# Small GpSimd operations for the decays, late selection, rotary cosine products from PSUM on VectorE, shorter norms, and pads between tiles, in a two-layer hybrid encoder

## The chip, the core and the metric

The kernel runs on one core of a Trainium2 chip. A core has TensorE (PE, matrix products), VectorE (DVE), ScalarE (ACT), GpSimd (POOL) and SyncE (SP, which here only issues transfers), each with an instruction queue of its own that is worked off in order; they meet at semaphores. SBUF is the on-chip memory with 128 partitions; PSUM takes the results of PE. The metric is the device time of one execution in microseconds (us), the median of several runs.

## What is computed

256 tokens of width 1024 in float32 go through two layers and a last RMSNorm:

```python
for l in range(DEPTH):                                   # 2
    h = rmsnorm(x, norm1_g[l])
    (r_q, r_k, r_v, r_g, d_q, d_k, d_v, d_z, d_b, d_a, gate_raw) = split_cols(h @ w_in[l])
    q, k = rotary(r_q), rotary(r_k)                      # 4 heads of 128
    o = retention_bidir(q, k, r_v)                       # fixed decays gamma_h^|n-m|
    y_ret = groupnorm(o) * silu(r_g)
    qkv = silu(centred_dwconv(concat(d_q, d_k, d_v)))    # 5 taps; 8 heads of 128
    dq, dk = l2norm(q part), l2norm(k part)
    g = -exp(a_log) * softplus(d_a + dt_bias)            # decays, per token, head, direction
    od = gated_delta_bidir(dq, dk, dv, beta, g)          # two directions, chunks of 128
    y_dn = rmsnorm(od) * silu(d_z)
    merged = sig(gA) * (y_ret @ w_proj_ret) + sig(gB) * (y_dn @ w_proj_dn)
    x = x + merged @ w_out
    x = x + square(relu(rmsnorm(x) @ w_ff1)) @ w_ff2
return rmsnorm(x, final_g)
```

`rotary` gives `[t1*cos - t2*sin, t1*sin + t2*cos]` of the halves t1, t2 of a head. In each chunk the delta rule needs `dec[i, j] = exp(gc_i - gc_j)` where j is before i (after it, for the other direction) and 0 elsewhere, gc being the running sum of g; it multiplies the k-k products (strictly before) and the q-k products (before or at). Then it solves a unit triangular system of 128 by 128 for each chunk, head and direction.

## The kernel before

**Products.** Weights are float32 and come by SP's transfers in pieces of 512 KB, `wrawc` (128 x 4 x 256) or `wraw` (128 x 2 x 512), three buffers in turn. `split` makes two reduced-precision parts of each piece: `whi` (ACT, L180) and the rest `wlo` (DVE, L181). The activations are kept in such parts too (`hTh`, `hTl` for the first norm's result, `h2h`, `h2l` for the second's, both transposed), and each product is three matmuls: hi*hi, lo*hi, hi*lo. There are two forms. `chan_pair` (L215 to L217) holds a 128 x 128 block of weights in the array and streams 256 tokens past it, 48 matmuls for a pair of output blocks: the names are `pcd` (the convolved columns), `pcrq` (rotary columns), `pcga`, `pcgb` (gates), `pcpr`, `pcpd` (projections; they read `yr` and `yd` in place of hT) and `pcf` (FF1). `tok_chunk` (L197 to L199) holds a block of activations and streams 512 columns of weights: `parv`, `parg`, `padz`, `pawo` (reads `mT`) and `paf` (FF2; reads `fh`, `fl`). There are 4608 of the first kind and 1536 of the second.

**Order.** The code is written by stages, and a scheduler that knows of priorities sets the order on each engine; weight transfers and splits are put ahead of other work. In a layer it goes: norm and transposes; gates and decays; conv columns of half 0 (4 heads), rotary columns beside them; half 1; values; the solve; the levels; outputs; projections; `pawo`; norm; FF1; FF2.

**Decays.** `gates_small` brings the running sums to all partitions by DMA as tiles `E` (128 x 2 directions x 2 chunks x 4 heads x 128, one for each half of the heads). For each direction POOL subtracts the partition's own sum (L330, one 128 x 1024 operation with a broadcast operand), then sets the wrong side to -1e30 (L334), and ACT takes one exponential for each half (L341). `delta_kk` multiplies: `A` from the k-k products, `sA` and E (L448), and E itself becomes the q-k products times E (L450). POOL copies four blocks of A into `W` (L459).

**Norm factors.** `half_inputs` collects squares in `ssq` (DVE L393 adds EPS), takes the power -0.5 on POOL (`powm`, L130, result `rs`), and makes `irk`, `rq` and `sA` on DVE (L398 to L405). `normed` does the same for tokens: ACT squares (L139), DVE adds the two halves and scales (L141, L142), POOL takes the power (L130), DVE scales the tokens (`xn`, L145), PE transposes (`pstn`, L167).

**Rotary.** In `retention`, for each of 16 heads of `pcrq` ACT copies the PSUM block to `ru` (L648), DVE multiplies the two exchanged halves by the sine table into `rw` (L650), POOL multiplies `ru` by the cosine table (L651) and adds (L652).

**Solve and levels.** `delta_solve` gathers the diagonal 32 x 32 blocks through DRAM (`gd`, then `Gm`), sets `X` to -Gm with ones on the diagonal (L468, L469), and runs 30 steps on DVE. X and its transpose go out by DMA (`xd`, `xtd`, L480, L481) and come back as some 40 small transfers into `dd`, `D` and `DT`; `delta_levels` then combines blocks with PE (`ps_y`, `ps_m`).

The parts of the program that the diff touches:

## Time and profile before

| | |
|---|---|
| timed runs (3) | 1135.25 us median, 1132.84 to 1136.71 |
| the profiled execution | 1128.0 us, span 1126.3 us |
| mean granted PE clock | 0.982 |
| busy PE / DVE / ACT / POOL | 1082.3 / 765.7 / 599.5 / 195.2 us |
| weight loads of PE (PEld) | 1003.9 us, beside the matmuls |
| transfers | 188.43 MB, 167 GB/s in the mean |

In the views of the profile, a group of instructions is written as line, engine, operation, output <- inputs, shape; buffer numbers are left out. "Busy" of PE counts a matmul from its start to the start of the next where they overlap, so 96% means that nearly every moment belongs to some matmul. In a window's row stand its limits and length, then for each engine the busy time and the count of instructions, then the clock that PE was granted, the transfers' share and their rate. A wait's row has the waiting instruction, what it waited for, the sum in us, how often, and the longest. A stage can be found in time by its names: the rotary and decay stage of layer 0 lies at 50 to 110 us and of layer 1 at 600 to 680, the levels at 205 to 240 and 760 to 795.

### The profile page before, as it was taken

Reading aid. Unit: us, or ns where it says so; the run is one execution under the profiler, and the core shown is the slowest. Engines: PE = TensorE matmul, PEld = TensorE weight load, DVE = VectorE, ACT = ScalarE, POOL = GpSimd, SP = SyncE. Lnnn points to the kernel's source line nnn. Section 1 sums busy time; section 2 is a strip of 40 time slices with the busy share of each in tenths; the row PEclk is TensorE's granted clock in tenths of the full one; section 3 lists DMA queues with packets and bytes.
Section 4 is the critical chain, followed back from the end, with each engine's and each line's share of the span. In section 5 each row is a group of like instructions: output and inputs, shape, how many; then the busy total and the mean of one; then the engine's idle time right before and its main releaser. Section 6 shows DMA issues by size and latency. Waiting matters only on the chain. (4 is left out here: it accounts for less than half of the span.)

```text
span 1126.3 us, 19629 instructions
## 1 busy us (share of the span) xinstructions
PE 1082.3 (96%) x7564; PEld 1003.9 (89%) x7564; DVE 765.7 (68%) x1359; ACT 599.5 (53%) x1046; POOL 195.2 (17%) x193
## 2 busy tenths in 40 slices
PE   6988999999999999999989899999999999999997
PEld 5988888989999899988879898989999989999885
DVE  4998999646576666644468898994657566666453
ACT  5986654433364566533359865454334556555342
POOL 2065200100002043300020751001001012332000
PEclk9999999989999999999999899999999999999999
DMA  6565675453545466556556556655444565655662
GB/s 211 160 182 157 173 211 150 114 158 97 153 145 183 157 203 182 177 191 211 171 165 177 161 162 193 187 154 135 124 142 113 173 204 165 192 185 188 188 194 104
DMA packets 175759, 188.43 MB, mean 167 GB/s; under 512 B 36240, under 2 KB 137010, under 8 KB 175666
## 3 DMA queue, kind: packets, MB, share of 16 engines
q1 hardware_dynamic: 174288, 185.17, 55.0%
q10 hardware_dynamic: 1378, 2.02, 0.5%
q8 instruction: 59, 0.97, 0.4%
q14 instruction: 34, 0.28, 0.1%
HBM read 181.85 MB, written 5.31 MB: 166 GB/s over the span
## 5 line engine op out<-in xcount | busy, mean ns | idle before, releaser
L181 DVE TENSOR_TENSOR wlo<-wrawc,whi 128x1024 fp32r<-128x1024 f32 x192 | 240.7, 1254 | 117.3 <-ACT whi L180 113.3
L180 ACT ACTIVATE whi<-wrawc 128x1024 fp32r<-128x1024 f32 x192 | 202.7, 1057 | 150.0 <-PE pcpr L216 25.3
L181 DVE TENSOR_TENSOR wlo<-wraw,whi 128x1024 fp32r<-128x1024 f32 x128 | 158.2, 1236 | 111.7 <-ACT whi L180 111.6
L180 ACT ACTIVATE whi<-wraw 128x1024 fp32r<-128x1024 f32 x128 | 135.5, 1059 | 172.3 <-PE paf L199 92.0
L216 PE MATMUL pcf<-h2l,whi 128*128 128x256 f32 x512 | 143.8, 283 | 0.0
L217 PE MATMUL pcf<-h2h,wlo 128*128 128x256 f32 x512 | 143.0, 283 | 0.0
L215 PE MATMUL pcf<-h2h,whi 128*128 128x256 f32 x512 | 142.0, 284 | 0.0
L217 PE MATMUL pcd<-hTh,wlo 128*128 128x256 f32 x384 | 110.8, 292 | 0.9 <-DVE wlo L181 0.9
L215 PE MATMUL pcd<-hTh,whi 128*128 128x256 f32 x384 | 110.3, 291 | 0.0
L216 PE MATMUL pcd<-hTl,whi 128*128 128x256 f32 x384 | 109.8, 287 | 0.0
L199 PE MATMUL paf<-whi,fl 128*128 128x512 f32 x256 | 100.8, 394 | 0.0
L198 PE MATMUL paf<-wlo,fh 128*128 128x512 f32 x256 | 100.7, 394 | 0.0
L216 PEld LDWEIGHTS pcf<-h2l,whi 128*128 128x128 f32 x512 | 98.2, 192 | 0.0
L217 PEld LDWEIGHTS pcf<-h2h,wlo 128*128 128x128 f32 x512 | 98.0, 192 | 0.0
L215 PEld LDWEIGHTS pcf<-h2h,whi 128*128 128x128 f32 x512 | 97.1, 192 | 0.0
L197 PE MATMUL paf<-whi,fh 128*128 128x512 f32 x256 | 90.2, 392 | 0.0
L832 POOL TENSOR_TENSOR fz<-fz 128x256 f32<-128x256 f32 x64 | 66.6, 1042 | 117.7 <-ACT fz L831 116.7
L215 PEld LDWEIGHTS pcd<-hTh,whi 128*128 128x128 f32 x384 | 73.9, 194 | 1.1 <-issue 0.2
L217 PEld LDWEIGHTS pcd<-hTh,wlo 128*128 128x128 f32 x384 | 73.5, 193 | 1.6 <-DVE wlo L181 1.2
L216 PEld LDWEIGHTS pcd<-hTl,whi 128*128 128x128 f32 x384 | 74.1, 193 | 0.4
L363 DVE SCALAR_TENSOR_TENSOR cacc<-pcd,cw,cacc 128x255 f32<-128x255 f32 (+1 forms) x144 | 67.1, 475 | 5.7 <-ACT cac L359 4.7
L197 PEld LDWEIGHTS paf<-whi,fh 128*128 128x128 f32 x256 | 48.1, 188 | 11.0
(268 smaller groups left out, 2637.6 us busy)
## 6 DMA issues: line engine op xcount, KB each, us to landing
wrawc<-in_w_in_dram SPq DMA_DIRECT2D x96, 512.0 KB, 3.8
wrawc<-in_w_ff_dram SPq DMA_DIRECT2D x64, 512.0 KB, 3.7
wraw<-in_w_ff_dram SPq DMA_DIRECT2D x64, 512.0 KB, 3.7
wraw<-in_w_in_dram SPq DMA_DIRECT2D x48, 512.0 KB, 3.7
wrawc<-in_w_proj_ret_dram SPq DMA_DIRECT2D x16, 512.0 KB, 3.4
wrawc<-in_w_proj_dn_dram SPq DMA_DIRECT2D x16, 512.0 KB, 3.4
wraw<-in_w_out_dram SPq DMA_DIRECT2D x16, 512.0 KB, 3.7
E<-rowd SPq DMA_DIRECT2D x16, 256.0 KB, 5.3
```

What stands on the lines that cost most here:

```text
L180: A.activation(hv, raw, AF.Copy)
L181: V.tensor_tensor(lv, raw, hv.bitcast(F32), ALU.subtract)
L197: T.matmul(ps[t], lhsT=a, rhs=wh[:, kk, :], start=k == 0, stop=False)
L198: T.matmul(ps[t], lhsT=a, rhs=wl[:, kk, :], start=False, stop=False)
L199: T.matmul(ps[t], lhsT=b, rhs=wh[:, kk, :], start=False, stop=k == nk - 1)
L215: T.matmul(ps[i], lhsT=wh[:, kk, c], rhs=a, start=k == 0, stop=False)
L216: T.matmul(ps[i], lhsT=wh[:, kk, c], rhs=b, start=False, stop=False)
L217: T.matmul(ps[i], lhsT=wl[:, kk, c], rhs=a, start=False, stop=k == KT - 1)
L363: V.scalar_tensor_tensor(a[:, o], ps[i][:, q], wk(k), a[:, o], ALU.mult, ALU.add)
L832: G.tensor_tensor(z2, z, z, ALU.mult)
```

## The change

Five things:

1. Decays: POOL's four 128 x 1024 subtractions with a broadcast operand in each layer become 32 operations of 128 x 128, one for each chunk, head and direction, that subtract a per-partition value and take the minimum with 0. The selection goes away from in front of the exponential; it stands in `delta_kk`, behind the copies into W, and sets the wrong side of the finished products to 0.
2. Rotary: `ru` is made by one DVE product that reads PSUM and the cosine table; ACT's copy and POOL's product are gone.
3. Norms: the squares are scaled as they are taken, so that one DVE step adds the halves and EPS, in `normed` (first norms) and in the last norm.
4. X is set to zero and ones on POOL ahead of time; five DVE operations copy the strict triangle of -Gm, which replace one whole negation and a memset.
5. Pads: `x1`, `cw1` and `hTl1` are allocated 448, 96 and 128 bytes longer in each partition, and used as before. All that is allocated behind them moves. In the two built programs, the places within a partition, modulo 512 bytes, are:

| tile | before | after |
|---|---|---|
| `whi`, `wlo` | 128 | 224 |
| `hTh`, `hTl`, `h2h`, `h2l` | 128 | 160 |
| `yr`, `yd` | 0 | 160 |
| `mT` | 0 | 160 |
| `fh`, `fl` of layer 0 / layer 1 | 0 / 64 | 160 / 224 |

So the distance weights minus activations, modulo 512, goes from 0 (hT, h2) and +128 (yr, yd) to +64 in all products of 256 columns; in those of 512 columns the distance activations minus weights goes from 0 (hT), -128 (mT, fh of layer 0) and -64 (fh of layer 1) to -64 (hT, mT, fh of layer 0) and 0 (fh of layer 1).

```diff
@@ -58,7 +58,9 @@
 
     SEQ = "11111011101101"
 
-    xh = [hp.tile([P, NT, 512], F32, tag=f"x{j}", name=f"x{j}") for j in range(2)]
+
+    xh = [hp.tile([P, NT * 512 + 112 * j], F32, tag=f"x{j}", name=f"x{j}")[:, :NT * 512]
+          .rearrange("p (t c) -> p t c", t=NT) for j in range(2)]
     cc = cst.tile([P, C_END - C_GAM], F32, tag="cc", name="cc")
     prow = sm.tile([P, 4, P], F32, tag="junk", name="prow")
     rows1, rows2, crow = prow[:16, 0], prow[:34, 1], [prow[:CK * 24, 2 + l] for l in range(DEPTH)]
@@ -105,7 +107,7 @@
 
     gT = cst.tile([P, 16], F32, tag="gT", name="gT")
     gT2 = cst.tile([P, 34], F32, tag="gT2", name="gT2")
-    cw = [cst.tile([P, CK * 24], F32, tag=f"cw{l}", name=f"cw{l}") for l in range(DEPTH)]
+    cw = [cst.tile([P, CK * 24 + 24 * l], F32, tag=f"cw{l}", name=f"cw{l}")[:, :CK * 24] for l in range(DEPTH)]
 
     def columns(dst, src, n):
         ps = aux.tile([P, 512], F32, tag="aux", name="ps_g")
@@ -136,10 +138,9 @@
             ss = sm.tile([P, 2], F32, tag="ss", name="ss1")
             for j in range(2):
                 junk = sm.tile([P, 512], mybir.dt.bfloat16, tag="djunk", name="junk1", bufs=1)
-                A.activation(junk, xh[j][:, t, :], AF.Square, accum_out=ss[:, j:j + 1])
+                A.activation(junk, xh[j][:, t, :], AF.Square, scale=D ** -0.5, accum_out=ss[:, j:j + 1])
             r = sm.tile([P, 1], F32, tag="r1", name="r1")
-            V.tensor_tensor(r, ss[:, 0:1], ss[:, 1:2], ALU.add)
-            V.tensor_scalar(r, r, 1.0 / D, EPS, ALU.mult, ALU.add)
+            V.tensor_scalar(r, ss[:, 0:1], ss[:, 1:2], EPS, ALU.add, ALU.add)
             powm(r, r, 1)
             for j in range(2):
                 V.tensor_scalar(dst[j][:, t, :], xh[j][:, t, :], r, None, ALU.mult)
@@ -218,7 +219,8 @@
         return ps
 
     def halves(tag, p, nm, dt=F32R):
-        return [p.tile([P, 4, S], dt, tag=f"{tag}{j}", name=f"{nm}{j}") for j in range(2)]
+        return [p.tile([P, 4 * S + (32 * j if tag == "hTl" else 0)], dt, tag=f"{tag}{j}", name=f"{nm}{j}")
+                [:, :4 * S].rearrange("p (k s) -> p k s", k=4) for j in range(2)]
 
     hT_hi, hT_lo = None, None
     for l in range(DEPTH):
@@ -326,13 +328,12 @@
                     for c in range(NT):
                         DQ.dma_start(
                             E[:, c], rowd[d, c, d, HH * hf:HH * hf + HH, :].partition_broadcast(P))
-                    i0 = 8 * d + HH * hf
-                    G.tensor_tensor(E, E, gc[:, :, i0:i0 + HH].unsqueeze(3).broadcast_to([P, NT, HH, P]),
-                                    ALU.subtract)
-                    ev = E.rearrange("p c h i -> p (c h) i")
-                    sg = 1 if d == 0 else -1
-                    G.affine_select(ev, ev, pattern=[[0, 8], [sg, P]], base=0, channel_multiplier=-sg,
-                                    compare_op=ALU.is_ge, fill=-1e30)
+
+                    for c in range(NT):
+                        for h in range(HH):
+                            u = 8 * d + HH * hf + h
+                            G.tensor_scalar(E[:, c, h, :], E[:, c, h, :], gc[:, c, u:u + 1], 0.0,
+                                            ALU.subtract, ALU.min)
             Ws = [dl.tile([P, 8, P], F32, tag="W", name="W", bufs=2) for hf in range(2)]
             for hf in range(2):
                 G.memset(Ws[hf], 0.0)
@@ -458,6 +459,11 @@
             for d, b, c in PAIRS:
                 G.tensor_copy(sc["W"][hf][blk[b], :, blk[c]], Av[d][blk[b], :, blk[c]])
             DQ.dma_start(sc["gd"][64 * hf:64 * hf + 64].rearrange("(u b) (j i) -> (b j) u i", b=4, i=32), adg)
+            for d in range(2):
+                ev = E[d].rearrange("p c h i -> p (c h) i")
+                sg = 1 if d == 0 else -1
+                G.affine_select(ev, ev, pattern=[[0, 8], [sg, P]], base=0, channel_multiplier=-sg,
+                                compare_op=ALU.is_ge, fill=0.0)
             q.update(E=E, Av=Av)
 
         def delta_solve():
@@ -465,8 +471,14 @@
             Gm = dl.tile([P, 32, 32], F32, tag="G", name="Gm")
             DQ.dma_start(Gm, sc["gd"].rearrange("q (j i) -> q j i", i=32))
             X = dl.tile([P, 32, 32], F32, tag="X", name="X")
-            V.tensor_scalar(X, Gm, -1.0, None, ALU.mult)
-            V.memset(X.rearrange("p a b -> p (a b)")[:, 0:1024:33], 1.0)
+            xf, gf = (t.rearrange("p a b -> p (a b)") for t in (X, Gm))
+            G.memset(X, 0.0)
+            G.memset(xf[:, 0:1024:33], 1.0)
+
+            for n in (16, 8, 4, 2, 1):
+                xs, gs = (bass.AP(tensor=f.tensor, offset=f.offset + n, ap=[f.ap[0], [66 * n, 16 // n], [32, n], [1, n]])
+                          for f in (xf, gf))
+                V.tensor_scalar(xs, gs, -1.0, None, ALU.mult)
             for j in range(1, 31):
                 n = 31 - j
                 tm = sm.tile([P, 256], F32, tag="stm", name="stm", bufs=1)
@@ -645,10 +657,9 @@
                     ps = chan_pair(wl_[:, off + 256 * i:off + 256 * (i + 1)], hT_hi, hT_lo, "rq")
                     for e in range(2):
                         h = 2 * i + e
-                        A.activation(u[:, h], ps[e], AF.Copy)
+                        V.tensor_tensor(u[:, h], ps[e], rot[:, 0], ALU.mult)
                         for a, b in (halfs, halfs[::-1]):
                             V.tensor_tensor(w_[a, h], ps[e][b], rot[b, 1], ALU.mult)
-                        G.tensor_tensor(u[:, h], u[:, h], rot[:, 0], ALU.mult)
                         G.tensor_tensor(t_[:, h], u[:, h], w_[:, h], ALU.add)
                 qk.append(t_)
             qT, kT = qk
@@ -843,7 +854,7 @@
                 V.scalar_tensor_tensor(xv, ps[t], rr2[:, t:t + 1], xv, ALU.mult, ALU.add)
                 if last:
                     A.activation(fin.tile([P, 512], mybir.dt.bfloat16, tag="fj", name="fj"), xv, AF.Square,
-                                 accum_out=fss[:, t, j:j + 1])
+                                 scale=D ** -0.5, accum_out=fss[:, t, j:j + 1])
                     if j == 0:
                         V.tensor_tensor(xg[:, t, :], xv, fg[:, :512], ALU.mult)
         if last:
@@ -852,8 +863,7 @@
             o = fin.tile([P, NT, D], F32, tag="o", name="o")
             for t in range(NT):
                 rt, ts = r[:, t:t + 1], slice(t * P, (t + 1) * P)
-                V.tensor_tensor(rt, fss[:, t, 0:1], fss[:, t, 1:2], ALU.add)
-                V.tensor_scalar(rt, rt, 1.0 / D, EPS, ALU.mult, ALU.add)
+                V.tensor_scalar(rt, fss[:, t, 0:1], fss[:, t, 1:2], EPS, ALU.add, ALU.add)
                 powm(rt, rt, 1)
                 V.scalar_tensor_tensor(o[:, t, 512:], xh[1][:, t, :], rt, fg[:, 512:], ALU.mult, ALU.mult)
                 A.activation(o[:, t, :512], xg[:, t, :], AF.Copy, scale=rt)
```

The order on POOL in layer 0, from the decays to the rotary sums, before (`rs` is the power that `half_inputs` of half 0 waits for):

```order
L330 TENSOR_TENSOR E<-E,gx 128x1024 x2
L334 AFFINE_SELECT E<-E 128x1024
L330 TENSOR_TENSOR E<-E,gx 128x1024
L334 AFFINE_SELECT E<-E 128x1024
L130 TENSOR_TENSOR rs<-ssq,mh 128x16
L330 TENSOR_TENSOR E<-E,gx 128x1024
L334 AFFINE_SELECT E<-E 128x1024 x2
L651 TENSOR_TENSOR ru<-ru,rot 128x256 x2
L652 TENSOR_TENSOR rT_1059<-ru,rw 128x256 x2
```

and after:

```order
L335 TENSOR_SCALAR E<-E,gx 128x128 x32
L132 TENSOR_TENSOR rs<-ssq,mh 128x16
L663 TENSOR_TENSOR rT_1075<-ru,rw 128x256 x4
L663 TENSOR_TENSOR rT_1710<-ru,rw 128x256 x3
L132 TENSOR_TENSOR rs<-ssq,mh 128x16
L663 TENSOR_TENSOR rT_1710<-ru,rw 128x256
L460 COPY W<-A_730 32x8x32 x2
L465 AFFINE_SELECT E<-E 128x1024
L460 COPY W<-A_731 32x8x32 x2
L465 AFFINE_SELECT E<-E 128x1024
```

The 32 small operations all stand ahead of the first `rs`, where before one subtraction and two selections came behind it; the cosine products are gone, and the four selections come among the copies into W.

The order on DVE in layer 0, from the sum of squares of half 0 (`ssq`) to the first use of its power (`irk`), before:

```order
L393 TENSOR_SCALAR ssq<-ssq 128x16
L363 SCALAR_TENSOR_TENSOR cacc<-pcd_870,cw_104,cacc 128x255
L363 SCALAR_TENSOR_TENSOR cacc<-pcd_870,cw_104,cacc 128x254
L364 TENSOR_TENSOR cacc<-cacc,cac_940 128x254
L181 TENSOR_TENSOR wlo<-wrawc,whi 128x1024
L363 SCALAR_TENSOR_TENSOR cacc<-pcd_964,cw_104,cacc 128x255 x2
L363 SCALAR_TENSOR_TENSOR cacc<-pcd_964,cw_104,cacc 128x254
L181 TENSOR_TENSOR wlo<-wrawc,whi 128x1024
L364 TENSOR_TENSOR cacc<-cacc,cac_1027 128x254
L363 SCALAR_TENSOR_TENSOR cacc<-pcd_965,cw_104,cacc 128x255 x2
L398 TENSOR_TENSOR irk<-ssq,rs 128x8
```

and the end of the same piece after, where `ssq` stands thirty rows further up:

```order
L660 TENSOR_TENSOR ru<-pcrq_1146,rot 128x256
L662 TENSOR_TENSOR rw<-pcrq_1146,rot 64x256 x2
L660 TENSOR_TENSOR ru<-pcrq_1147,rot 128x256
L662 TENSOR_TENSOR rw<-pcrq_1147,rot 64x256 x2
L182 TENSOR_TENSOR wlo<-wrawc,whi 128x1024 x2
L364 SCALAR_TENSOR_TENSOR cacc<-pcd_1216,cw_104,cacc 128x255 x2
L364 SCALAR_TENSOR_TENSOR cacc<-pcd_1216,cw_104,cacc 128x254
L182 TENSOR_TENSOR wlo<-wrawc,whi 128x1024
L365 TENSOR_TENSOR cacc<-cacc,cac_1279 128x254
L364 SCALAR_TENSOR_TENSOR cacc<-pcd_1217,cw_104,cacc 128x255 x2
L364 SCALAR_TENSOR_TENSOR cacc<-pcd_1217,cw_104,cacc 128x254
L399 TENSOR_TENSOR irk<-ssq,rs 128x8
```

Two splits stood between `ssq` and `irk`; now eight do, with the rotary products of four heads (`ru` and `rw`) and another conv block.

The order on SP in layer 0, around the transfers of the solved blocks, before:

```order
L190 DMA wraw<-in_w_in_dram 128x2x512 x8
L208 DMA wrawc<-in_w_in_dram 128x4x256 x5
L480 DMA xd<-X 128x1024
L481 DMA xtd<-XT 128x1024
L502 DMA dd<-xd 32x8x32
L503 DMA dd<-xd 32x8x32
```

and after:

```order
L191 DMA wraw<-in_w_in_dram 128x2x512 x8
L209 DMA wrawc<-in_w_in_dram 128x4x256 x7
L492 DMA xd<-X 128x1024
L209 DMA wrawc<-in_w_in_dram 128x4x256
L493 DMA xtd<-XT 128x1024
L514 DMA dd<-xd 32x8x32
```

`xd` goes out two weight pieces later, and one more piece stands between it and `xtd`.

## The prediction

> **What bounds the kernel now.** I read the page first, then the windows of 50 us, then what PE waited for, then windows of single tiles, then the engines' own timelines at the one stage that has holes. The page says that TensorE is the bound almost everywhere:
>
> ```profile
> span 1126.3 us, 19629 instructions
> PE 1082.3 (96%) x7564; PEld 1003.9 (89%) x7564; DVE 765.7 (68%) x1359; ACT 599.5 (53%) x1046; POOL 195.2 (17%) x193
> ```
>
> The sum below is made against this execution: 1128.0 us, with a span of 1126.3. It lies 7.25 us under the median of the timed runs (1135.25), so I carry the difference over to that median. PE is idle for 1126.3 − 1082.3 = 44 us only; everything else is matmuls, one behind the other. So a change can win in two ways: fill the 44 us, or make a matmul's slot shorter. The windows say where the idle time lies (column PE busy, of 50 us each):
>
> ```profile
> core 0: us, PE busy (x) PEld busy (x) DVE busy (x) ACT busy (x) POOL busy (x), PEclk, DMA share, GB/s
> 50.00:100.00 50.00, 45.45 (x354) 43.51 (x353) 47.32 (x96) 43.02 (x105) 27.77 (x22) 1.00 0.62 179
> 100.00:150.00 50.00, 47.43 (x290) 43.07 (x289) 41.99 (x87) 27.82 (x49) 13.29 (x13) 0.97 0.65 179
> 200.00:250.00 50.00, 46.72 (x420) 45.27 (x419) 25.63 (x50) 21.04 (x39) 4.30 (x4) 0.90 0.50 133
> 600.00:650.00 50.00, 46.08 (x347) 44.96 (x346) 44.91 (x90) 44.08 (x115) 22.33 (x16) 0.90 0.58 170
> 650.00:700.00 50.00, 49.27 (x320) 45.12 (x319) 48.64 (x103) 29.94 (x55) 18.56 (x19) 1.00 0.63 175
> 750.00:800.00 50.00, 47.81 (x415) 45.33 (x414) 29.58 (x63) 21.13 (x39) 3.59 (x4) 0.93 0.57 149
> ```
>
> The rotary-and-decay stage (50 to 150 and 600 to 700) leaves 4.55 + 2.57 + 3.92 + 0.73 = 11.8 us idle: there DVE is 90 to 97% busy and POOL has its only dense stretch. The levels of the block solve (200 to 250, 750 to 800) leave 3.28 + 2.19 = 5.5. The waits of PE name what ended the holes:
>
> ```profile
> engine line waited for: us in total, times, longest us
> PE pstn L167 <- DVE xn L145: 9.3, 4, 4.1
> PE ps_kt L384 <- ACT kq L382: 6.5, 6, 2.2
> ...
> PE ps_m L525 <- DMA DT<-xtd: 3.3, 2, 2.4
> PE pcrq L215 <- DVE cacc L363: 2.8, 3, 2.0
> PE pcrq L215 <- DVE rw L650: 2.6, 1, 2.6
> PE pcrq L217 <- DVE wlo L181: 1.8, 3, 1.1
> ```
>
> **Part 1, the pads.** They move tiles, and add no instruction. By the addresses in the two built programs, the distance between weights and moving data in a partition's memory, taken modulo 512 bytes, was 0 for 3840 of the 4608 products with 256 columns (all that read hT or h2) and +128 for the 768 of `pcpr` and `pcpd`; it becomes +64 for all of them. Did the distance matter before? Both kinds have a window in which PE did nothing else (20 us, busy time, count):
>
> ```profile
> 400.00:420.00 20.00, 20.00 (x169) 20.00 (x168) 2.59 (x7) 1.00 0.68 208
> 340.00:360.00 20.00, 20.00 (x171) 20.00 (x171) 2.50 (x6) 1.00 0.58 181
> ```
>
> The first is `pcf` (distance 0), the second `pcpd` (+128). A window holds every matmul that overlaps it, so the spacing is the window and one matmul's 0.28 us, over the count: 20.28/169 = 120.0 ns and 20.28/171 = 118.6 ns. The same shape at full clock is 1.4 ns cheaper off the distance 0. That is the nearest row for +64, and I take it: 3840 × 1.4 ns = 5.4 us gained, and nothing for the 768.
>
> The 512-column products are the second row that speaks on this: `paf` in layer 0 had the distance −128, in layer 1 −64, and `parv` 0:
>
> ```profile
> 500.00:560.00 60.00, 60.00 (x259) 48.62 (x259) 1.40 (x2) 1.00 0.60 193
> 1050.00:1110.00 60.00, 60.00 (x264) 49.21 (x263) 1.41 (x2) 1.00 0.58 184
> 119.00:125.00 6.00, 6.00 (x28) 4.94 (x28) 0.00 (x0) 1.00 0.56 167
> ```
>
> With 0.39 us for one: 60.39/259 = 233.2, 60.39/264 = 228.8, and 6.39/28 = 228.2 ns (a short window, good to a few ns). Here a distance other than 0 is no cheaper. After the pads the 480 layer-0 products of `paf` and `pawo` go from −128 to −64 (480 × −4.4 ns = −2.1 us), the 96 of `pawo` in layer 1 too (−0.4), `paf` in layer 1 goes to 0 (384 × −0.6 = −0.2), and the 576 on hT go from 0 to −64 (576 × +0.6 = +0.3). Together −2.4; I take −2, with ends −4 and +1.
>
> For the 256-column products the ends are wider, since no row shows +64. Below: a wide slot carries 512 columns in 228.2 ns, so 114.1 for 256 columns; if the pads free the narrow slot of all that it pays beyond this, 3840 × 5.9 + 768 × 4.5 ns = −26 us. Above: in the 512-column rows a distance other than 0 cost 0.6 to 5.0 ns more; half the columns, half of it, 2.5 × 4608 = +12 us.
>
> [...]
>
> **Part 2, the decays.** In the rotary stage POOL and DVE run at once, and DVE pays (start and duration in us, first DVE's rows, then POOL's of the same time):
>
> ```profile
> 61.64 0.41 DVE L364 TENSOR_TENSOR cacc<-cacc,cac 128x254 f32<-128x254 f32 x1
> ...
> 62.36 1.21 DVE L181 TENSOR_TENSOR wlo<-wrawc,whi 128x1024 fp32r<-128x1024 f32 x1
> ...
> 64.00 1.62 DVE L364 TENSOR_TENSOR cacc<-cacc,cac 128x254 f32<-128x254 f32 x1
> 65.55 2.92 DVE L181 TENSOR_TENSOR wlo<-wrawc,whi 128x1024 fp32r<-128x1024 f32 x1
> ...
> 71.49 2.10 DVE L181 TENSOR_TENSOR wlo<-wrawc,whi 128x1024 fp32r<-128x1024 f32 x1
> ...
> 77.31 0.95 DVE L398 TENSOR_TENSOR irk<-ssq,rs 128x8 f32<-128x8 f32 x1
> ```
>
> ```profile
> 63.45 3.93 POOL L330 TENSOR_TENSOR E<-E,gx 128x1024 f32<-128x1024 f32 x2 [50.58 <-DMA E<-rowd]
> ...
> 71.24 1.27 POOL L334 TENSOR_SCALAR_AFFINE_SELECT E<-E 128x1024 f32<-128x1024 f32 x1
> 72.49 3.87 POOL L130 TENSOR_TENSOR rs<-ssq,mh 128x16 f32<-128x16 f32 x1
> ```
>
> The split L181 took 1.21 us alone and 2.92 and 2.10 beside L330; L364, 0.41 at 61.64, took 1.62 at 64.00. And `rs` stands behind the decays in POOL's queue, while DVE's queue stops at `irk` until `rs` is there, with the next splits behind it. This is where `pcrq <- cacc`, `<- wlo` and most of `ps_kt <- kq` come from. The groups give the prices (busy, mean ns):
>
> ```profile
> L330 POOL TENSOR_TENSOR E<-E,gx 128x1024 f32<-128x1024 f32 x8 | 16.4, 2060 | 98.7 <-DMA E<-rowd 96.9 <-DVE cacc L363 1.8
> L651 POOL TENSOR_TENSOR ru<-ru,rot 128x256 f32<-128x256 f32 x16 | 15.4, 970 | 10.4 <-ACT ru L648 10.3
> L334 POOL TENSOR_SCALAR_AFFINE_SELECT E<-E 128x1024 f32<-128x1024 f32 x8 | 11.0, 1384 | 0.0
> L459 POOL COPY W<-A 32x256 f32<-32x256 f32 x16 | 10.3, 641 | 31.0 <-DVE A L448 30.6
> L677 DVE TENSOR_TENSOR sT<-ps_st,cc 128x256 f32<-128x256 f32 x16 | 6.2, 416 | 1.8 <-PE ps_st L675 1.7
> L648 ACT ACTIVATE ru<-pcrq 128x256 f32<-128x256 f32 x16 | 6.0, 374 | 0.0
> ```
>
> Before, each layer had 4 × 2.06 + 4 × 1.38 = 13.8 us of POOL ahead of the last exponential. After, it has 32 small operations of 128x128. No such operation is in the trace: an eighth of L330 is 0.26 us, an eighth with a fixed cost is bounded by the small COPY of 0.64, so 8.3 to 20.5 us; I take 0.4, nearer to the row of the same engine and data, or 12.8 us. The four selections (5.5 us) come behind the W copies, where the window from 100 to 150 above has POOL busy for 13.3 of 50 us; I cost them at nothing. If they were late, the output products behind the levels would wait. Ahead of the first `rs` stood three subtractions and two selections, 8.9 us, and now all 12.8: `rs` comes some 4 us later. But DVE reads it (at `irk`) six splits later, and a split feeds 24 slots of 120 ns: 17 us. So that stop is gone unless the small operations take over (8.9 + 17)/32 = 0.8 us, and what is late next is the first `ps_kk`, whose products now stand later in PE's queue as well.
>
> **Part 3, the rotary products.** 16 `ru` products leave POOL (15.4 us) and 16 copies leave ACT (6.0). DVE gets 16 × 0.416, by L677, which also reads PSUM and one table: 6.7 us, 3.3 in each layer, in a stage where it is the second bound. Against it stands what contention cost DVE there (1.7 + 1.2 + 0.9 us in three of the rows above alone), of which POOL's lost 13 us should take about half. A `pcrq` bank is now let go by three products of one engine in a row, 0.42 + 2 × 0.42 us, where ACT took the first part: up to +0.4 us for each of 8 pairs, hidden where the next pair's bank is free.
>
> Parts 2 and 3 together work on the 11.8 idle us. I take two thirds back, −8. Ends: all of it, −12; and +3, if the 3.3 us of DVE land on the waits of one layer and nothing is won.
>
> **Part 4, norms and X.** Each norm loses one DVE step (the chain ahead of `pstn`, 9.3 us of waits above):
>
> ```profile
> 569.88 0.15 DVE L142 TENSOR_SCALAR r<-r 128x1 f32<-128x1 f32 x1
> ```
>
> Two tokens' tiles in each of two norms, 4 × 0.15, and less than that where the two overlap: −0.5 us. X built by triangles replaces a negation, whose time is covered by PE work, which stands between the solve and the levels. But the order has XT one split and more later, a 512 KB weight transfer between `xd` and `xtd` in SP's queue, and PE's filler ahead of the levels some 3 us of matmuls shorter in layer 0. The wait `ps_m <- DT<-xtd` (3.3) can grow: I take +1, ends −2 and +4.
>
> **The sum.** −5.4 − 2 − 8 − 0.5 + 1 = −14.9: 1113 for the profiled execution, 1120 for the median.
>
> **Rivals.**
> - *The pads do nothing for the 256-column slot.* For it: 228.2 against 228.8 ns in the wide products. Then −8 − 2 − 0.5 + 1 = −9.5: 1126.
> - *The pads do much.* If 118.6 is a quarter of the way out of a collision and +64 leaves it, the slot comes near 114.1 ns: −26 by the end worked out above, with −9.5: 1135.25 − 35.5 = 1100. Against it: no row of this shape is under 118.6.
> [...]
> - *Slower, by the distance.* If +64 behaves as −128 does in the wide products (+5.0 ns in a slot), 4608 × 2.5 to 5.0 ns = +12 to +23, less 9.5: 1138 to 1149. It decides from a slot of about 122 ns; below that the decay stage pays for it.
>
> **Chances.** My forecast 0.37, pads at nothing 0.18, pads much 0.18, eaten gain 0.14, slower by the distance 0.13. A measurement of this kernel tells 0.3% (3.4 us) from no change. The first three are faster, as is the eaten gain in a fifth of its cases: 0.76. The rest of that one is "same", with some of the distance rival: 0.12. Slower keeps 0.12. The range leaves out the upper part of the distance rival and what lies beyond the large gain: 1099 to 1137. The likeliest case alone would have 1113 to 1126: the sum with the decay term at −12 and the levels at −2, or at −2 and +1.
>
> **What would show it.** The spacing of `pcf` in a window of its own (118.6 forecast; 120.0, under 116 or over 122 name a rival). L181 between 60 and 80 us near 1.21 instead of 2.92. PE's waits on `cacc`, `rw`, `wlo` and `kq` in the rotary stage down from 13.7 us to about 5, and no wait on `ps_kk`. L335 at 0.3 to 0.5 us. `ps_m <- DT<-xtd` not over 5 us. What would make me most wrong is a slot that moves by more than 2 ns either way, for there are 4608 of them.

## The result and the profile after

| | before | after | ratio, 95% interval |
|---|---|---|---|
| timed beside each other, first time (4 and 4 runs) | 1134.05 us | 1119.93 us | 0.9877 [0.9849, 0.9906] |
| again on another occasion (11 and 6 runs) | 1130.36 us | 1121.86 us | 0.9920 [0.9896, 0.9943] |
| the profiled executions | span 1126.3 | span 1121.1 | |

The forecast was 1120 us in a range of 1099 to 1137. The time came out, but its large terms did not: the pads brought more than their term and the rotary and decay stage next to nothing, as the profile and the experiments show. The page of after, first lines:

```profile
span 1121.1 us, 19644 instructions
PE 1077.8 (96%) x7564; PEld 998.3 (89%) x7564; DVE 761.1 (68%) x1375; ACT 594.9 (53%) x1030; POOL 217.5 (19%) x237
```

PE's idle time, 1121.1 − 1077.8 = 43.3 us, is what it was (44.0). PE's busy time fell by 4.5. The windows that were shown of before, now of after:

```profile
50.00:100.00 50.00, 45.42 (x362) 44.57 (x361) 39.96 (x80) 41.94 (x98) 35.32 (x37) 0.93 0.64 186
100.00:150.00 50.00, 49.35 (x306) 43.90 (x305) 49.29 (x110) 28.77 (x50) 15.58 (x17) 1.00 0.60 167
200.00:250.00 50.00, 47.30 (x402) 46.49 (x401) 25.17 (x51) 22.20 (x41) 2.64 (x4) 0.83 0.56 147
600.00:650.00 50.00, 46.33 (x380) 45.62 (x378) 40.45 (x80) 43.19 (x105) 34.93 (x36) 0.97 0.66 191
650.00:700.00 50.00, 47.50 (x289) 41.96 (x288) 49.56 (x113) 28.00 (x51) 16.52 (x19) 1.00 0.55 157
750.00:800.00 50.00, 47.86 (x396) 46.59 (x395) 26.87 (x60) 21.65 (x40) 3.31 (x4) 0.82 0.58 153
```

The rotary and decay stage is idle for 4.58 + 0.65 + 3.67 + 2.50 = 11.4 us against 11.8: next to nothing won. And the clock column of the levels fell from 0.90 and 0.93 to 0.83 and 0.82. PE's waits, the first six rows:

```profile
PE ps_kt L385 <- ACT kq L383: 11.8, 7, 4.2
PE pstn L168 <- DVE xn L146: 8.4, 4, 4.9
PE ps_g L114 <- POOL ident L94: 6.0, 1, 6.0
PE ps_y L527 <- DMA dd<-xd: 3.2, 2, 2.2
PE pcd L216 <- DVE rw L662: 2.4, 4, 1.5
PE ps_m L537 <- DVE D L539: 1.5, 3, 0.5
```

`pcrq <- cacc`, `<- rw` and `<- wlo` are gone (7.2 us), as forecast. `ps_kt <- kq` rose from 6.5 to 11.8 with two single waits of 4.2 and 3.7, and `pcd <- rw` is new: a wait for DVE's rotary products again, now by the conv columns. Last, the slots of the narrow products, in windows that hold one tile alone (`pcf`, then `pcpd`):

```profile
400.00:420.00 20.00, 20.00 (x172) 20.00 (x171) 2.77 (x8) 1.00 0.67 201
342.00:352.00 10.00, 10.00 (x87) 10.00 (x86) 1.25 (x3) 1.00 0.61 194
```

20.28/172 = 117.9 ns (120.0 before) and 10.28/87 = 118.2 (118.6 before). These two tiles moved by 2.1 and 0.4 ns. Over all starts of matmuls in the trace that follow one of the same kind, the mean slot of the 4608 narrow products went from 119.7 to 116.4 ns, which is 15.3 us, and that of the 1536 wide ones from 230.0 to 230.3, which is −0.5.

The trace also holds the stretches in which PE had half its clock. They sum to 41.8 us before and 61.4 after. In both kernels a narrow product followed the one before it after 213 ns in the median there, and outside them after 120 (before) and 117 (after). If PE works all through such a stretch, half of it is lost at the most: 9.8 us more after. This closes the sum of the two profiled executions: −15.3 + 0.5 (slots) − 0.7 (idle) + 9.8 (clock) = −5.7, against 1121.1 − 1126.3 = −5.2.

### The profile page after: what moved, and what is told of

The parts are those of the page before. It is cut to its first block, busy times and chain, and to the rows that moved or that the text cites. A ratio compares the mean times of both kernels' runs of the same rounds, so it can differ in the third digit from the quotient of the medians.

```text
span 1121.1 us, 19644 instructions
## 1 busy us (share of the span) xinstructions
PE 1077.8 (96%) x7564; PEld 998.3 (89%) x7564; DVE 761.1 (68%) x1375; ACT 594.9 (53%) x1030; POOL 217.5 (19%) x237
## 4 chain that ended last, share of the span: by engine, by line
PE 41%; POOL 3%; DVE 3%; SPq 1%; DMA 1%; issue 1%; ACT 1%; POOLq 0%
PE pcf L218 3%; PE pcf L216 3%; PE pcf L217 3%; PE paf L200 3%; PE paf L198 3%; PE paf L199 3%; POOL E L335 3%; PE pcd L216 1%; PE pcd L217 1%; PE pcd L218 1%; DVE wlo L182 1%; PE pcpr L217 1%; PE pcpr L216 1%; PE pcpr L218 1%; PE parg L199 1%; PE pcpd L218 1%
## 5 line engine op out<-in xcount | busy, mean ns | idle before, releaser
L182 DVE TENSOR_TENSOR wlo<-wrawc,whi 128x1024 fp32r<-128x1024 f32 x192 | 238.1, 1241 | 111.9 <-ACT whi L181 110.6
L181 ACT ACTIVATE whi<-wrawc 128x1024 fp32r<-128x1024 f32 x192 | 202.4, 1057 | 141.6 <-PE pcpr L217 22.1
L181 ACT ACTIVATE whi<-wraw 128x1024 fp32r<-128x1024 f32 x128 | 135.6, 1059 | 183.2 <-PE paf L200 91.5
L218 PE MATMUL pcd<-hTh,wlo 128*128 128x256 f32 x384 | 108.5, 288 | 0.0
L335 POOL TENSOR_SCALAR E<-E,gx 128x128 f32<-128x128 f32 x64 | 58.9, 940 | 95.9 <-DMA E<-rowd 50.1
```

Of the source, the lines that this page charges most:

```text
L181: A.activation(hv, raw, AF.Copy)
L182: V.tensor_tensor(lv, raw, hv.bitcast(F32), ALU.subtract)
L218: T.matmul(ps[i], lhsT=wl[:, kk, c], rhs=a, start=False, stop=k == KT - 1)
L335: G.tensor_scalar(E[:, c, h, :], E[:, c, h, :], gc[:, c, u:u + 1], 0.0, ALU.subtract, ALU.min)
```

## The experiments

All times are medians; the kernel before had 1131.8 us beside e1 to e4, 1131.7 beside e5 to e8 and 1130.4 beside e9 to e12. The last columns are from the trace of the one profiled execution: the mean slots, and half of the time at half clock. That execution was the longest of those timed for the changed kernel's first measurement, e1, e6 and e10, so their clock loss is at the upper end of what their runs had. Slots, clock loss and PE's idle time (41.8 to 50.6 us) together give each span's difference from before to within 3.2 us, and to within 5 for e3. e1 to e8 ran on one chip and e9 to e12 on another, so kernels of the two groups are compared by their ratios.

| kernel | us | ratio, 95% interval | narrow, wide slot (ns) | clock loss (us) |
|---|---|---|---|---|
| before | 1131.8 | 1 | 119.7, 230.0 | 20.9 |
| e1 pads only | 1117.5 | 0.9877 [0.9855, 0.9900] | 115.7, 230.1 | 29.7 |
| e2 all but the pads | 1127.4 | 0.9959 [0.9939, 0.9978] | 119.7, 229.9 | 21.7 |
| e3 big decays | 1125.1 | 0.9932 [0.9906, 0.9957] | 115.5, 230.4 | 29.5 |
| e4 two large operations | 1123.8 | 0.9940 [0.9918, 0.9962] | 115.4, 230.1 | 26.7 |
| e5 pads and rotary | 1122.9 | 0.9928 [0.9901, 0.9956] | 115.9, 230.2 | 28.5 |
| e6 rotary as before | 1126.8 | 0.9952 [0.9922, 0.9982] | 116.1, 230.1 | 34.0 |
| e7 pads, aligned wide products | 1114.0 | 0.9851 [0.9823, 0.9879] | 114.9, 228.0 | 24.8 |
| e8 map (one run) | 1127.6 | | 117.7, 230.8 | 23.1 |
| e9 the changed kernel again | 1121.9 | 0.9920 [0.9896, 0.9943] | 115.8, 230.4 | 27.5 |
| e10 one exponential | 1122.2 | 0.9924 [0.9896, 0.9952] | 115.3, 230.3 | 39.6 |
| e11 changed, aligned | 1118.9 | 0.9897 [0.9865, 0.9928] | 115.0, 228.0 | 26.1 |
| e12 one exponential, aligned | 1121.1 | 0.9901 [0.9868, 0.9934] | 116.2, 228.0 | 34.2 |

### The pads alone, and all but the pads

```diff
 e1: the kernel before, with the longer x1, cw1 and hTl1 of the change
 e2: the changed kernel, with x1, cw1 and hTl1 as before
```

> The kernel before with the three pads alone; the tiles then lie at the same distances as in the changed kernel. Theory A (the pads carry the whole gain; the decay and rotary parts cancel out): the slots of the 256-column products fall as in the changed kernel's trace (pcf 120.0 to 117.3 ns, pcd 119.6 to 115.7, pcpr 119.4 to 114.1), 15.3 us over all of them, less 0.5 us lost in the 512-column ones: 1134 - 14.7 = 1119 us, ratio 0.987. Theory B (the split of the prediction): the pads bring 7.4 us, 1127 us, ratio 0.9935.

> The changed kernel without the three pads. Theory A: the slots go back to 120.0 ns, and the rest of the change is worth nothing: 1134 us, the time of the kernel before, ratio 1.00. Theory B: what is left is the decay stage, the norms and the levels, 7.5 us: 1126.5 us, ratio 0.993. In both the holes of PE in the rotary and decay stage should be those of the changed kernel: two waits of ps_kt on kq of about 4 us each.

e1 gave 1117.5, e2 1127.4. The pads alone are worth 14.3 us, which is theory A's figure; all else alone is worth 4.4, more than A and less than B said. Added they would be 18.7; the whole change has 14.1, and 8.5 on the second occasion: the rest of the change brings nothing on top of the pads, and may cost up to 5 us. The slots of e2 are those of before to 0.1 ns (the same window of `pcf`):

```profile
400.00:420.00 20.00, 20.00 (x169) 20.00 (x168) 2.88 (x8) 1.00 0.64 198
```

In the same window e1 has 20.28/172 = 117.9 ns (its row with the columns of PE, PEld, DVE, ACT and POOL):

```profile
400.00:420.00 20.00, 20.00 (x172) 20.00 (x171) 14.52 (x17) 12.82 (x24) 8.85 (x9) 1.00 0.68 206
```

So the slots are the pads' work and nothing else's. Some loss of clock seems to come with the pads too: e1, with nothing but tiles moved, lost 29.7 us to half clock in its profile, 8.8 more than before, and the mean clock of its timed runs was 0.978 (6 runs) against 0.981 (26 runs of the kernel before). e2, without the pads, stayed at 0.981 (12 runs).

### What the small decay operations do

```diff
 e3: the changed kernel, with the decays of before
-  G.tensor_scalar(E[:, c, h, :], E[:, c, h, :], gc[:, c, u:u + 1], 0.0, ALU.subtract, ALU.min)  # x8
+  G.tensor_tensor(E, E, <gc broadcast>, ALU.subtract); G.affine_select(..., fill=-1e30)
 e4: large operations, late selection kept
+  G.tensor_tensor(E, E, <gc broadcast>, ALU.subtract); G.tensor_scalar(E, E, 0.0, None, ALU.min)
```

> The changed kernel with the decays of before: four 128x1024 subtractions and selections to -1e30 in a layer, ahead of the exponential; no late selection. Theory A (the small operations cost POOL 29.6 us a layer and stop ACT, and by that PE for 4.2 and 3.7 us; they give back what they save in contention): the two waits of ps_kt go, splits of 2 to 3 us beside POOL come back, the sum is within 3 us of the changed kernel, 1117 to 1123. Theory B (the small operations free DVE and that is worth 8 us): 1128 us. Theory C (the rotary products off POOL were the good part and the small operations are a loss): 1112 us.

> The changed kernel with two large operations in place of eight small ones: one 128x1024 subtraction with a broadcast operand, then one 128x1024 minimum with 0; the late selection stays. If the number of operations sets POOL's time (0.71 us each at the least), POOL needs 4 x (1.9 + about 1.1) = 12 us a layer instead of 29.6, the exponential finds its E ready, and the two waits of ps_kt (7.9 us) go: 1112 us, if DVE is not slowed; with the slow splits of before (1.7 + 0.9 us a layer and more) 1115 to 1120. If the amount of data sets it, as much POOL time as now and 1120 us.

First the changed kernel's own rows: POOL's group of the small operations, DVE's splits beside them, and ACT at the same time (start, duration):

```profile
L335 POOL TENSOR_SCALAR E<-E,gx 128x128 f32<-128x128 f32 x64 | 58.9, 940 | 95.9 <-DMA E<-rowd 50.1 <-DVE wlo L182 45.7
```

```profile
63.96 1.23 DVE L182 TENSOR_TENSOR wlo<-wrawc,whi 128x1024 fp32r<-128x1024 f32 x1
...
67.00 1.23 DVE L182 TENSOR_TENSOR wlo<-wrawc,whi 128x1024 fp32r<-128x1024 f32 x1
...
71.35 1.23 DVE L182 TENSOR_TENSOR wlo<-wrawc,whi 128x1024 fp32r<-128x1024 f32 x1 [1.44 <-ACT whi L181]
```

```profile
75.17 1.28 ACT L342 ACT_TABLE_LOAD   x1
78.20 1.91 ACT L342 ACTIVATE E<-E 128x2048 f32<-128x2048 f32 x1 [1.75 <-POOL E L335]
80.02 1.04 ACT L181 ACTIVATE whi<-wrawc 128x1024 fp32r<-128x1024 f32 x1
81.07 1.28 ACT L383 ACT_TABLE_LOAD   x1
82.37 0.42 ACT L383 ACTIVATE kq<-cacc 128x256 f32<-128x256 f32 x1
```

```profile
82.84 0.69 PE L385 MATMUL ps_kt<-ident,kq 128*128 128x128 f32 x2 [4.17 <-ACT kq L383]
```

DVE no longer pays for POOL: its splits take 1.23 us beside the small operations (one in layer 1 took 1.35). POOL pays instead: a small operation takes 0.71 us at the least, up to 1.94 beside a split and 0.94 in the mean, 30 us of POOL in a layer. The exponential stands ahead of the next `kq` in ACT's queue. ACT changes its table at 75.17, waits 1.75 us for POOL, and starts `kq` at 82.37, 5.6 us after DVE had finished its input (L365, at 76.74). PE waits 4.2 us for it, and 3.7 in layer 1.

In e3 the contention is back (DVE, same stretch):

```profile
62.17 1.21 DVE L182 TENSOR_TENSOR wlo<-wrawc,whi 128x1024 fp32r<-128x1024 f32 x1
...
65.36 2.92 DVE L182 TENSOR_TENSOR wlo<-wrawc,whi 128x1024 fp32r<-128x1024 f32 x1
...
71.30 2.11 DVE L182 TENSOR_TENSOR wlo<-wrawc,whi 128x1024 fp32r<-128x1024 f32 x1
```

So the 2.92 goes with the subtraction of two tensors; POOL being busy is not enough for it. By the ratios e3 is 6 us over the changed kernel's first measurement (theory B), and 1 us over its second (theory A): the timing leaves it open. In the profile PE is idle for 46.8 us against 43.3, and the timed runs had a mean clock of 0.9746 against 0.9788 and 0.9765, so what difference there is may lie in both. The long wait of `ps_kt` is gone in e3 (5.7 us in all, the longest 1.8), but `pcrq <- cacc` (4.8) and `pcd <- wlo` (3.3) took its place. e4 refutes my guess that the count of operations sets the price:

```profile
L335 POOL TENSOR_SCALAR E<-E 128x1024 f32<-128x1024 f32 x8 | 26.3, 3287 | 0.0
L333 POOL TENSOR_TENSOR E<-E,gx 128x1024 f32<-128x1024 f32 x8 | 17.0, 2130 | 98.9 <-DVE cacc L364 51.2 <-DMA E<-rowd 47.6
```

A minimum with a constant took 3.29 us in the mean for 1024 columns, longer than the subtraction of two tensors (2.13): an eighth of it, for 128 columns, is 0.41 us. So POOL needed 21.7 us a layer where I had expected 12. The two long waits of `ps_kt` went (the longest is 1.9 us), but splits of 1.5 to 2.9 us beside POOL came back (those of `wrawc` took 1.260 us in the mean, 1.241 in the changed kernel), PE was idle for 48.7 us, and the time is 1123.8, over both figures expected.

### The rotary products

```diff
 e5: before, with the pads and: V.tensor_tensor(u[:, h], ps[e], rot[:, 0], ALU.mult)
 e6: the changed kernel, with ru by ACT copy and POOL product
```

> The kernel before with the pads and with the rotary cosine products on DVE from PSUM; decays, norms and X as before. The pads alone gave 0.9877 (1117.5 us), and the changed kernel with the big decays 0.993 (1125.1 us, mean clock 0.975 against 0.978). Theory A (the rotary products on DVE are what costs that kernel its 7 us: DVE carries 3.3 us more a layer beside slow splits, and the levels come later and in a slower clock): 0.993, 1125 us. Theory B (it is X, the norms or chance in the levels' clock): 0.988, 1118 us.

> The changed kernel with the rotary products of before: ACT copies ru, POOL multiplies it by the cosine table. Theory A (the rotary part moves work from POOL, which the small operations fill for 29.6 us, to DVE, and pays only with them): POOL's products queue behind the small operations, the sums rT and the retention's later parts come late, but PSUM is let go by ACT as before; DVE has 3.3 us less a layer; between 1117 and 1121 us, ratio 0.987 to 0.990. Theory B (POOL's longer queue reaches PE): rs comes later by up to 8 x 0.74 us, ps_kk and the solve with it, 1123 us or more.

e5, 1122.9, is 5.4 us over the pads alone, as theory A said; e6, 1126.8, is 4 to 8 over the changed kernel by the ratios, as theory B said: POOL's 30 us of small operations stand ahead of the cosine products, and in its profile PE, idle for 50.6 us, waits for a new thing:

```profile
PE ps_kt L385 <- ACT kq L383: 11.9, 9, 4.0
PE pstn L168 <- DVE xn L146: 8.3, 4, 4.9
PE ps_g L114 <- POOL ident L94: 6.0, 1, 6.0
PE ps_kk L445 <- DVE E L451: 5.0, 3, 2.3
```

On top of the pads alone (0.9877) the rotary part costs 5.8 us by the ratios, all the rest without it 8.5, and everything together 0 to 5. So the two parts seem to belong together, but the intervals of e5 and e6 overlap that of the changed kernel's second measurement, so this is not shown.

### Distances: alignment and a map

```diff
 e7: the kernel before with the pads, and
+  D64h[1] 64 bytes longer (mT moves by 64)
+  spare = ff.tile([P, 16], ...)   # layer 0: fh and fl move by 64
 e8: the kernel before, no pads, and
-  wp.tile([P, 1024], F32R, tag="whi")          # wlo too
+  wp.tile([P, 1024 + 16], F32R, tag="whi")[:, :1024]
```

> The kernel before with the three pads, and 64 bytes more ahead of mT's hi and lo parts and of layer 0's fh and fl, so that pawo and paf have the distance 0 in both layers and the 256-column products stay at +64. From the slots (512 columns: 227 ns at 0, 229 to 233 at other distances): 384 x 6 ns in paf of layer 0 and 192 x 2 to 5.5 ns in pawo, 2.7 to 3.4 us under the pads alone: 1114.5 us, ratio 0.985. If the slot of the wide products doesn't depend on the distance: as the pads alone, 1117.5.

> A map: the kernel before with 64 bytes more behind each of the six buffers of whi and wlo, so that each piece of weights lies at another distance from the activations (in pcf 128, 192, 256 for whi and 320, 384, 448 for wlo; in pcpd 256, 320, 384 and 448, 0, 64). If the slot is a function of the distance modulo 512: 120.0 ns stays where the distance is 0, 118.6 at 128, about 113 to 118 at 64 and some value for each of the others. If what matters is only whether the distance is a multiple of a smaller step, all of pcf falls to 113 to 118 ns (the sum 5 to 20 us under the kernel before), or, if 64 is the only good one, none does.

e7 is the fastest kernel of this study: 1114.0 us, 3.5 under the pads alone by the medians and 2.9 by the ratios, with intervals that overlap. `paf` of layer 0, where before had 259 matmuls in 60 us, then `pcf` of e7:

```profile
490.00:550.00 60.00, 60.00 (x266) 49.73 (x265) 1.41 (x2) 1.00 0.63 193
...
400.00:420.00 20.00, 20.00 (x179) 20.00 (x178) 2.62 (x7) 1.00 0.67 209
```

60.39/266 = 227.0 ns against 233.2, and 20.28/179 = 113.3 ns at +64 against 120.0 at 0: the wide products want the distance 0, the narrow ones do not. Over all wide products the mean fell from 230.1 to 228.0 ns, 3.2 us. Here the weights stayed in their places and only the activations moved. e8 shows that +64 is not the only way off the 120 ns. With six distances from 128 to 448 in turn `pcf` fell from 120.0 to 20.28/173 = 117.2 ns in layer 0, and to 117.9 in layer 1:

```profile
400.00:420.00 20.00, 20.00 (x173) 20.00 (x172) 2.60 (x7) 1.00 0.69 210
950.00:970.00 20.00, 20.00 (x172) 20.00 (x171) 3.26 (x9) 1.00 0.67 205
```

The six had 116.8 to 119.8 ns in the mean, if the time from one start to the next is put down to the second product (114.7 to 119.6 if to the first). But a product's own distance does not set its slot: the products of `pcpd` and `pcpr` that e8 puts at the distance 0, between neighbours at other distances, had 117.7 and 117.9 ns by the two counts, and not 120. So the 120.0 ns at 0 and the 113 to 118 at +64 are shown for stretches in which all products share one distance, and why the addresses matter stays open. The wide products of e8, off 0 for the most part, lost 0.8 ns in the mean, and one run of 1127.6 does not tell it from the kernel before (1126.2 to 1136.1).

### The changed kernel again, one exponential, and all together

```diff
 e9: no edit
 e10: the changed kernel with E of both halves in one tile
-  for hf in range(2): A.activation(Es[hf], Es[hf], AF.Exp)
+  A.activation(Eb, Eb, AF.Exp)
 e11: the changed kernel with e7's 64 bytes;  e12: e10 with e7's 64 bytes
```

> The changed kernel once more, beside the others of this call. In its first profile the 256-column slots of pcpd stayed at 117.8 ns and those of pcf at 117.3, where other kernels with the same distances had 113.3 to 113.6 in one layer or both. If the slot is a matter of the phase into which loads and matmuls fall in one execution, these values change between the two profiles of the same program; if the program sets it, they are the same, within 0.2 ns. Time in both cases 1118 to 1120 us, ratio 0.988.

> The changed kernel with one exponential over the decays of both halves, in place of two; ACT then meets it after the kq activations that the first one held up. Theory A (the wait of ACT for POOL's small operations is what ate the gain of the decay stage): the two waits of ps_kt on kq of 4.2 and 3.7 us go, the one exponential finds its data late and is waited for by A once a layer, 1 to 2 us; 5 us under the changed kernel, 1114 us, ratio 0.983. Theory B (the wait moves: A and the solve come later, or the freed time is lost in the levels' slower clock): within 2 us of the changed kernel.

> The changed kernel with the 64 bytes ahead of mT and of layer 0's fh and fl, which with the pads alone brought 3.5 us (1117.5 to 1114.0). If slots add up with the rest of the change: 1116 us, ratio 0.985; if the levels' clock or a phase takes it: 1118 to 1120.

> Both: the one exponential and the 64 bytes. If both theories hold, 5 + 3 us under the changed kernel: 1111 us, ratio 0.980, under the pads with the alignment alone (1114.0). If only the alignment holds: 1116.

e9: the same program, another execution. `pcf` of layer 1 in the first profile of after, then in the second:

```profile
950.00:970.00 20.00, 20.00 (x172) 20.00 (x171) 2.59 (x7) 1.00 0.70 210
```

```profile
950.00:970.00 20.00, 20.00 (x179) 20.00 (x178) 2.95 (x8) 1.00 0.69 207
```

117.9 against 113.3 ns. At the distance +64 the unbroken stretches of narrow products, `pcf` and `pcpd`, settle into one of two slots, and stay there for a whole stage; all other tiles agreed within 0.8 ns, and `parg` of layer 0 within 1.8. One execution can hold both, as e9 does in the two layers (`pcf` of layer 0 had 117.2). For `pcf` of one layer the two are 3.5 us apart, as much as lies between the medians of e1 and e7.

e10 refutes the remedy. The first wait of `kq` went, but the one exponential, with its change of table and its wait for POOL, now holds up the splits behind it (first ACT's row, then PE's waits):

```profile
91.93 3.63 ACT L342 ACTIVATE E<-E 128x4096 f32<-128x4096 f32 x1 [1.73 <-POOL E L336]
```

```profile
PE pstn L168 <- DVE xn L146: 7.8, 3, 4.9
PE pcrq L216 <- ACT whi L181: 6.4, 2, 4.8
PE ps_g L114 <- POOL ident L94: 6.0, 1, 6.0
PE ps_kt L385 <- ACT kq L383: 5.7, 6, 2.2
PE pcrq L218 <- DVE wlo L182: 4.5, 3, 1.8
```

11.8 became 5.7 + 6.4 + 4.5, and the clock loss rose to 39.6 us in this execution; over the timed runs the mean clock was 0.972 against 0.9765 in e9. e11 and e12 are 3 and 1 us under e9 and e10, less than their intervals can tell, and stay over e7.

## Why the prediction was right, and where it was not

**The time** was right by luck: the pads' term was too small by about half and the stage's too large by nearly all, and the two misses cancelled. −7.4 and −8 were forecast; the pads brought −14.3 (e1), and all else brought −4.4 without them (e2) and 0 to +5 on top of them. Of the signs that the prediction named, L181's 1.23 us, no wait on `ps_kk`, and `ps_m <- DT<-xtd` under 5 us came true. The waits of the rotary stage on `kq` and `rw`, 11.8 + 2.4 us and not 5, and L335, 0.94 us and not 0.3 to 0.5, did not.

**Part 1, narrow slots.** Forecast −5.4, from 118.6 ns taken for +64. Measured −15.3 and −17.7 us in two profiles (slots of 113.3 to 118 ns), with −14.3 timed for the pads alone. The direction was read rightly from the two rows of 120.0 and 118.6; the size failed where the nearest row was taken for the value, while +64 had two values, 113.3 and 117.8 ns, near the low end of its range (114.1) and under the row that it took. In e1 nothing but addresses was changed, and the 4608 slots got shorter by 4.0 ns in the mean (119.7 to 115.7).

**Part 1, wide slots.** Forecast −2, measured +0.5. I had put the difference between 233.2 and 228.8 down to −128 against −64; after the pads layer 0's `paf` had −64 and stayed at 233.3, and only the distance 0 (e7) took it to 227.0. −64 has no one price: `pawo`, at the same places in both kernels, had 229.0 ns in e1 and 232.5 in the changed kernel. Why stays open.

**Part 2, decays.** The step that failed is the price of the small operation: 0.4 us taken in a range of 0.26 to 0.64, 0.71 at the least and 0.94 in the mean measured, 30 us of POOL in a layer in place of 12.8. I took a price near an eighth of another operation; e4 shows that a minimum with a constant is slower than that operation also when it is one large piece. The point from which I said that it would hurt, 0.8 us, was passed, but another waiter was met first: not DVE's `irk`, but ACT's exponential, with `kq` behind it, which the prediction did not name. That DVE is freed was right (2.92 to 1.23 us); that the price moves to POOL's own operations was not foreseen.

**Part 3, rotary.** The 16 products took 0.417 us (0.416 forecast). On top of the pads alone they cost 5.8 us (e5); the 8 us that I gave the two parts together became 4.4 for all but the pads (e2), and nothing or a loss with the pads (e1 against the changed kernel). The wait for a bank that DVE's products hold, which the prediction called hidden where the next bank is free, may be `pcd <- rw` (2.4 us, and 3.8 in e9). The "POOL's lost 13 us" does not come out of the prediction's own rows (15.4 + 2 × (13.8 − 12.8) = 17.4), and POOL lost nothing: its busy time rose from 195.2 to 217.5 us. Why the two parts are worth less beside the pads was not separated from the clock's loss.

**Part 4.** The levels' waits on transfers went from 0.3 + 3.3 (`ps_y`, `ps_m`) to 3.2 + 0, and to 3.8 + 1.3 in e9: −0.4 and +1.5, so the +1 was fair. What no term had is the clock there (0.90 and 0.93 before, 0.83 and 0.82 after).

**Rivals.** The eaten gain (0.14) came true in its result, 11.4 us idle in the stage against 11.8, by ACT's queue (`ps_kt <- kq` 11.8 us against 6.5) rather than by DVE's load; "the pads do much" came true by more than half. So the sum was right by two misses of opposite sign, and not by its working.

## What to carry to other kernels

Where matmuls follow one another without a hole, measure the slot of each kind in a window that holds only that kind, and try a few pads between weights and activations: here 672 bytes were worth 14 us, and 64 in two more places some 3 more, with no instruction of the computation changed. A cheap-looking rewrite for an idle engine is priced by that very operation in a trace, not by its data's share of another; and its result's reader may stand at the head of a queue in which others wait. Sum a change to a saturated engine in three accounts, slots, idle time and clock: here, in the padded kernels, the last gave back 4 to 19 us by the profiles, or 2 to 12 as an estimate from the mean clocks of the timed runs (1 minus the clock, times the time, less the same of the kernel before), of what the first had won.

## What the runs showed of the hardware

- Slots of products with 256 columns, in stretches that hold one distance: 120.0 ns at 0 modulo 512 (`pcf`), 118.6 at +128 (`pcpd`), and at +64 one of two, about 113.3 or 117.8, which can differ between layers and between executions. With 512 columns: 227 to 228 ns at 0, 229 to 233 at −64 and −128.
- In the traces of before and after, PE's clock was granted at 1.0 or at 0.5. The stretches at 0.5 had 3.4 (twice), 6.8 and 10.2 us (twice) before, and 3.4 (twice), 6.8, 17.1 and 23.9 us after: 1, 2, 3, 5 and 7 times 3.41. One more runs into the end of each trace. In after the two longest begin at 228.9 and 781.8 us, in the levels, where PE had been busy for 1.83 and 2.92 of the last 4 us. In the padded kernels' profiles the loss was 24.8 to 39.6 us against 20.9 and 21.7 in those without pads (23.1 in e8). Why was not shown.
- On POOL, an operation with a scalar per partition and a constant took 0.71 us at the least for 128 x 128, a minimum with a constant 3.29 in the mean for 128 x 1024, a subtraction of two tensors 2.06 to 2.26 in the mean for the same size. Beside DVE's subtraction of two tensors (the split) POOL paid in the first case (up to 1.94), and DVE in the last (2.92 against 1.21). By what they hinder each other was not shown.
